# The first modulation of a two-block DiT on one core: whole row blocks of the weights, plain fp32 products on four column tiles

## The chip, the cores and the metric

The kernel runs on one core of a Trainium2 chip. Its engines are TensorE (PE in the profile; PEld are its weight loads), VectorE (DVE), ScalarE (ACT), GpSimd (POOL) and SyncE (SP), which here only issues DMAs. The metric is the device time of one execution in microseconds (us).

## The reference

Two transformer blocks over 256 tokens x and 256 context tokens, width 1024. Each block begins with a modulation: six vectors for x and six for the context, products of silu(c) and silu(c_ctx) with w_mod. The first two of the six (shift and scale) modulate the norms that go into the token mixer:

```
silu_c  = silu(c);  silu_cc = silu(c_ctx)                       # 1024 each
mod_x = silu_c  @ w_mod[l] + b_mod[l]                           # w_mod[l]: 1024 x 6144, fp32
mod_c = silu_cc @ w_mod[l] + b_mod[l]
sh1x, sc1x, g1x, sh2x, sc2x, g2x = split(mod_x, 6)
hx = rmsnorm(x, norm_mix_w[l])   * (1 + sc1x) + sh1x
hc = rmsnorm(ctx, norm_mix_w[l]) * (1 + sc1c) + sh1c
mx, mc = token_mixer(hx, hc, ...)                               # starts with hx @ w_in, hc @ w_in
x = x + g1x * mx;  ...                                          # then a dense channel mixer,
                                                                # and in block 1 eight experts, top 2
```

The change is about the first 2048 columns of mod_x and mod_c of block 0: a product of a 2 x 1024 matrix with 1024 x 2048 weights (8.4 MB), without which no token of block 0 can be modulated.

## The kernel before

Products that need the precision of fp32 are made of rounded parts. A load brings a unit of weights of 128 x 1024 numbers (0.5 MB) into one of four places `raw` (`load_unit`, line 128). `split_unit` then makes `hi` on ScalarE (a rounded copy, L145) and `lo` = raw - hi on VectorE (L149), in rings of three places each. The rounded type (fp32r) lets TensorE take a product in one pass; three such products (`mm3`, L156 to L158) stand for one exact one.

The first modulation (L309 to L345) goes by columns: four chunks of 512 columns, and in each four units of 256 rows. The two vectors are kept in `cst` as four columns per block of 128 rows, rounded part and rest of each, so that one product of `hi` and one of `lo` with them (L337) give four rows of 512 sums. ScalarE copies those four rows out (L338) into `rows`, whose fifth row is the bias. Four small products with a matrix of ones and zeros, `sel` (L341), add rows 0, 1, 4 and rows 2, 3, 4 and turn the result into columns, `colps`; VectorE copies these to `modc` (L344). From `modc` come the factors `ac` (L351), and then the norms of the tokens are transposed (L290) and modulated, block by block of 128 columns, on ScalarE (L300, L303, L304) and VectorE (L301, L305). The context's two tiles of tokens come first (`h_first[0]`), those of x (`xs`, scaled by L280) later, between the first products of the mixer. These blocks (`hb`, in the ring `rb`) are what the mixer multiplies with the weights w_in, starting with the gate inputs and keys (`gates_keys`, PE mm L156 to L158).

The order of instructions on each engine is set by a scheduler from the program's order, priorities and the waits that it expects; `split_unit` has high priority. `behind(a, b)` keeps a load behind another one in SyncE's queue: in this part all loads are a chain, w_mod first, then w_in, x and constants. The loads of SyncE and ScalarE share eight completion semaphores (the order's rows call them DMAHW0 to DMAHW7); a load waits for the one before it on the same semaphore. The later modulations (`mod_chunk`, from L399) work in another way, on VectorE (L417), with a sum over partitions by one fp32 product (L423, L427).

Other places in memory that matter here: the rings `rr` and `rb`, of four places of 128 x 2048 fp32 numbers each. In the first 40 us `rr` holds little (gate parameters, the start of the later modulations), and `rb` is unused until the modulated blocks go there.

Of the kernel before, what the change touches and what calls it, by code (L numbers as in the profile page):

```python
# [16 lines left out]
OP = mybir.AluOpType  # L17
# [21 lines left out]
def host_consts():  # L39
# [15 lines left out]
    sel = np.zeros((5, 2))  # L55
    sel[[0, 1, 4], 0] = 1
    sel[[2, 3, 4], 1] = 1
# [14 lines left out]
def hybrid_kernel(ctx: ExitStack, tc: tile.TileContext, a: dict, out: bass.AP, dbg=None, upto="end"):  # L72
# [10 lines left out]
    # before the experts' weights: raw units of w_mod, gates, sums; blocks of transposed tokens  # L83
    turn = {"mraw": 0, "blk": 0}

    def ring(kind, i, dt):
        """one of the rings' places of 8 KB"""
        return ringp.tile([128, 4, 512], dt, name=f"{kind}{i}", tag=f"{kind}{i}")
# [6 lines left out]
    def blk(dt=F32R):  # L95
        """half of a place; two in a row share one"""
        k = turn["blk"]
        turn["blk"] += 1
        if k % 2 == 0:
            turn["pair"] = ring("rb", k // 2 % 4, dt)  # L100
        assert turn["pair"].dtype == dt
        return turn["pair"][:, k % 2 * 2:k % 2 * 2 + 2]
# [5 lines left out]
    # ------------------------------------------------------------------ weights  # L108
# [3 lines left out]
    def place_of(x, n, keep=False):  # L112
        """the next place of a kind; the experts' units have rings of their own, with some places for once"""
# [23 lines left out]
    def chained():  # L137
        """the first loads and the last ones keep the order of the trace"""
        return W["chain"] or places
# [20 lines left out]
    # ------------------------------------------------------------------ constants  # L160
    # the scalar engine's function tables change in the order of the trace
# [7 lines left out]
    class InOrder:  # L169
        """the engine's instructions keep the order of the trace among themselves"""  # L170
# [50 lines left out]
    sel = consts.tile([5, 2], F32, name="sel")  # L221
# [9 lines left out]
    cst = consts.tile([128, KB, 4], F32R, name="cst")  # L231
# [6 lines left out]
    rows = mx0.tile([5, 2048], F32, name="rows", tag="uh")  # L238
    nc.scalar.dma_start(rows[4:5, :], a["b_mod"][0:1, 0:2048])
# [6 lines left out]
    def rstd_of(ss, pool, first=None):  # L246
        """(sum of ss / D + EPS) ** -0.5 for [128, 1], with a Newton step; first: the first half's EPS + ss / D"""
# [11 lines left out]
    def rstd_newton(ss, first, pool, i):  # L259
        """(ss / D + first) ** -0.5 for [128, 1]: Newton steps from an integer guess"""  # L260
# [13 lines left out]
    def norm_tile(xt, pool, bufs=2, junk=None):  # L274
        """rmsnorm without its weight; in place where the squares have a place of their own"""
# [7 lines left out]
    def h_steps(xns, blks, acol, bcol, pool, tr, h32tag, off=0, mix=(0, 1)):  # L283
        """Two token tiles -> modulated, transposed, split into blks[kb][:, :, seq half]."""
# [23 lines left out]
    # ------------------------------------------------------------------ first modulation  # L308
    with tc.high_priority():  # L309
# [3 lines left out]
        nc.vector.tensor_copy(cst[:, :, 0], cs[:, 0:8])  # L313
        nc.vector.tensor_tensor(cst[:, :, 1], cs[:, 0:8], cst[:, :, 0].bitcast(F32), op=OP.subtract)
        nc.vector.tensor_copy(cst[:, :, 2], cs[:, 8:16])
        nc.vector.tensor_tensor(cst[:, :, 3], cs[:, 8:16], cst[:, :, 2].bitcast(F32), op=OP.subtract)
# [3 lines left out]
    colps = ps0.tile([128, 512], F32, name="colps", tag="sc", bufs=4)[:, :32].rearrange("p (a b) -> p a b", b=2)  # L320
    modc = {}
    modc[0] = modp.tile([128, 2, 16], F32, name="modc0")
    for ch in range(4):
        if ch == 1:
            for t in range(2):
                ins = nc.sync.dma_start(xin[t], a["ctx"][0, t * 128:(t + 1) * 128, :]).ins
                behind(ins, W["load"])
                W["load"] = ins
            junk = mx0.tile([128, D], F32, name="junk", tag="v0")
            xns = [norm_tile(xin[t], mx0, junk=junk) for t in range(2)]  # L330
        mps = ps0.tile([128, 512], F32, name="mps", tag="mm", bufs=4)[:4]
        for q in range(4):
            hl = split_unit(load_unit(wsrc(a["w_mod"][0], q * 256, 2, ch * 512, 512), (2, 512)))
            for k in range(2):
                kb = 2 * q + k
                for i, m in enumerate(hl):
                    nc.tensor.matmul(mps, cst[:, kb, :], m[:, k, :], start=(kb == 0 and i == 0), stop=(kb == 7 and i == 1))  # L337
        nc.scalar.activation(rows[0:4, ch * 512:(ch + 1) * 512], mps, AF.Copy)  # L338
        for j in range(4):
            b = ch * 4 + j  # L340
            nc.tensor.matmul(colps[:, b, :], rows[:, b * 128:(b + 1) * 128], sel, start=True, stop=True)  # L341
        if ch % 2:
            s = ch // 2
            nc.vector.tensor_copy(modc[0][:, :, s * 8:(s + 1) * 8],  # L344
                                  colps[:, s * 8:(s + 1) * 8, :].rearrange("p b x -> p x b"))  # L345

    def acols(l, which, mc, x):
        """columns (a, b) of the modulated norm; mc [128, 2, 16]: shift | scale"""
# [37 lines left out]
    # ------------------------------------------------------------------ later modulations  # L386
    gp = {}

    class later:
        """instructions that give way to the next ones traced"""  # L390
# [10 lines left out]
    def mod_chunk(l, col, n_src, rows_out=None, cols_out=None):  # L401
        """512 columns of w_mod[l] from col, for x (and ctx): on the vector engine, with the
        sum over partitions left to the tensor engine."""
# [29 lines left out]
    def g_mod(l, which, n_src):  # L433
        col = (2 if which == 1 else 5) * D
        if (l, which) == (1, 2):
            # as columns; rows are made of them when they are needed
# [22 lines left out]
    # ------------------------------------------------------------------ token mixer  # L459
# [1176 lines left out]
```

## Time and profile before

| | before |
|---|---|
| time, median of 3 runs | 1826.84 us (1826.77 to 1829.52) |
| the profiled execution | span of 1826.0 us from first to last instruction; the page gives no other time of its own, so what lies around the span is taken as 0.84 us from the median |
| TensorE busy | 1782.2 us (98%) |
| VectorE busy | 1470.1 us (81%) |
| ScalarE busy | 1084.2 us (59%) |
| DMA | 479 MB, mean 262 GB/s |

Busy time is an average over stages with different limits; the start of the program, about 42 us until the first modulated block, is a stage of its own. A matmul's record is longer than its share of the engine, since matmuls are pipelined: the distance from one start to the next counts. An fp32 product is two records, a rounded one is one.

### The profile page before, as it was taken

To read this page: it belongs to the slowest core of one execution; us is meant where nothing else is said; L and a number is where in the kernel's file an instruction comes from. 1 tells how busy PE (TensorE), PEld (TensorE's weight loads), DVE (VectorE), ACT (ScalarE), POOL (GpSimd) and SP (SyncE) were. 2 spreads that over 40 slices of the span, in tenths; PEclk is the share of its full clock that TensorE was granted. 3 is DMA by queue.
4 is the path that set the end of the run, shared out by engine and by line. 5 is a ranking of instruction groups with operands and counts; after the bars stand their busy time and mean duration, and the time that the engine had idled before them with its cause. 6 is when DMAs were issued, how large, how long until landed. Compare 5 with 4: busy or idle time off the path is not lost.

```text
span 1826.0 us, 22994 instructions
## 1 busy us (share of the span) xinstructions
PE 1782.2 (98%) x8724; PEld 1450.5 (79%) x8724; DVE 1470.1 (81%) x1537; ACT 1084.2 (59%) x1120; POOL 26.8 (1%) x51
## 2 busy tenths in 40 slices
PE   6999999999999999999999999999999999999997
PEld 2777888888888887877888888888888888888875
DVE  6788896786565577668889888898898898988997
ACT  6733454222212366547777777777777777777774
POOL 1000000000000000000000000000000000000000
PEclk9999999999999999999999999999999999999999
DMA  8534374556555345469999999999999999999972
GB/s 289 188 94 133 106 247 137 183 174 184 185 187 183 116 130 185 150 249 359 334 352 338 349 363 354 344 369 342 366 362 338 366 359 339 364 348 360 335 236 97
DMA packets 253159, 478.99 MB, mean 262 GB/s; under 512 B 11773, under 2 KB 65279, under 8 KB 253039
## 3 DMA queue, kind: packets, MB, share of 16 engines
q1 hardware_dynamic: 251440, 473.80, 75.1%
q10 hardware_dynamic: 1040, 2.72, 0.4%
q8 instruction: 70, 1.15, 0.3%
q0 software_dynamic: 560, 0.92, 0.2%
q14 instruction: 49, 0.40, 0.1%
HBM read 476.35 MB, written 1.05 MB: 261 GB/s over the span
## 4 chain that ended last, share of the span: by engine, by line
PE 92%; DVE 3%; ACT 2%; DMA 1%; issue 1%; ACTq 0%; DVEq 0%; POOLq 0%
PE h L1479 11%; PE h L1482 11%; PE h L1478 11%; PE mm L156 8%; PE mm L157 8%; PE mm L158 8%; PE y L156 8%; PE y L157 8%; PE y L158 8%; PE sc L1340 1%; PE sc L1460 1%; PE sc L584 1%; ACT hi L145 1%; PE mm L427 1%; DMA raw<-w_mod 1%
## 5 line engine op out<-in xcount | busy, mean ns | idle before, releaser
L177 DVE TENSOR_TENSOR rb<-raw,rb 128x2048 fp32r<-128x2048 f32 (+1 forms) x159 | 355.3, 2246 | 16.6 <-PE h L1479 11.0
L177 ACT ACTIVATE rb<-raw 128x2048 fp32r<-128x2048 f32 (+1 forms) x159 | 300.1, 1887 | 100.2 <-PE h L1482 65.6
L1479 PE MATMUL h<-rb,hg 128*128 128x512 f32 x896 | 351.4, 392 | 1.2 <-DVE rb L177 1.2
L145 ACT ACTIVATE hi<-raw 128x1024 fp32r<-128x1024 f32 x143 | 151.2, 1059 | 331.9 <-PE mm L157 100.7
L1478 PE MATMUL h<-rb,hg 128*128 128x512 f32 x670 | 262.9, 392 | 0.0
L149 DVE TENSOR_TENSOR lo<-raw,hi 128x1024 fp32r<-128x1024 f32 x143 | 174.7, 1223 | 103.8 <-ACT hi L145 102.4
L177 DVE TENSOR_TENSOR rb<-raw,part 128x2048 fp32r<-128x2048 f32 (+1 forms) x80 | 177.7, 2221 | 34.5 <-ACT part L177 21.4
L1479 PEld LDWEIGHTS h<-rb,hg 128*128 128x128 f32 x896 | 168.4, 188 | 38.8 <-DVE rb L177 3.8
L417 DVE SCALAR_TENSOR_TENSOR rr<-rr,cs,rr 128x512 f32<-128x512 f32 x256 | 181.8, 747 | 10.5 <-DMA rr<-b_mod 6.6
L1482 PE MATMUL h<-rb,hg 128*128 128x512 f32 x670 | 179.8, 390 | 1.6 <-DVE hg L177 1.6
L157 PE MATMUL y<-rb,ht 128*128 128x512 f32 x448 | 177.4, 396 | 0.0
L177 ACT ACTIVATE part<-raw 128x2048 fp32r<-128x2048 f32 (+1 forms) x80 | 148.9, 1861 | 34.3 <-PE y L158 33.3
L156 PE MATMUL mm<-hbk,hi 128*128 128x512 f32 (+1 forms) x456 | 167.3, 368 | 0.1
L157 PE MATMUL mm<-hbk,hi 128*128 128x512 f32 (+1 forms) x456 | 164.9, 362 | 1.1 <-DVE hbk L305 1.1
L158 PE MATMUL mm<-hbk,lo 128*128 128x512 f32 (+1 forms) x456 | 165.0, 362 | 0.0
L177 DVE TENSOR_TENSOR rb<-rr,rb 128x2048 fp32r<-128x2048 f32 (+1 forms) x68 | 150.0, 2208 | 11.9 <-ACT h L177 7.9
L177 ACT ACTIVATE rb<-rr 128x2048 fp32r<-128x2048 f32 (+1 forms) x68 | 126.3, 1857 | 38.9 <-PE h L1482 22.7
L1482 PEld LDWEIGHTS h<-rb,hg 128*128 128x128 f32 x670 | 125.7, 188 | 28.3 <-DVE hg L177 2.1
L1478 PEld LDWEIGHTS h<-rb,hg 128*128 128x128 f32 x670 | 125.9, 188 | 26.2 <-issue 0.2
L157 PEld LDWEIGHTS y<-rb,ht 128*128 128x128 f32 x448 | 84.3, 188 | 19.5 <-DVE rb L177 0.3
L156 PEld LDWEIGHTS mm<-hbk,hi 128*128 128x128 f32 x456 | 85.7, 188 | 16.5 <-issue 1.2
L157 PEld LDWEIGHTS mm<-hbk,hi 128*128 128x128 f32 x456 | 85.9, 189 | 16.0 <-DVE hbk L305 1.3
(355 smaller groups left out, 3143.8 us busy)
## 6 DMA issues: line engine op xcount, KB each, us to landing
raw<-moe_w SPq DMA_DIRECT2D x228, 1024.0 KB
rr<-moe_w SPq DMA_DIRECT2D x96, 1024.0 KB
rr<-w_mod SPq DMA_DIRECT2D x80, 512.0 KB
raw<-ffn_w SPq DMA_DIRECT2D x72, 512.0 KB
raw<-w_in SPq DMA_DIRECT2D x32, 512.0 KB
raw<-w_out SPq DMA_DIRECT2D x23, 512.0 KB
raw<-w_mod SPq DMA_DIRECT2D x16, 512.0 KB
raw<-moe_w SPq DMA_DIRECT2D x11, 512.0 KB
```

The costliest lines, as they stand in the source:

```text
L145: ins = nc.scalar.activation(hi, raw, AF.Copy).ins
L149: nc.vector.tensor_tensor(lo, raw, hi.bitcast(F32), op=OP.subtract)
L156: nc.tensor.matmul(ps, lh, rh, start=start, stop=False)
L157: nc.tensor.matmul(ps, lh, rl, start=False, stop=False)
L158: nc.tensor.matmul(ps, ll, rh, start=False, stop=stop)
L177: r = getattr(self.engine, name)(*args, **kw)
L417: nc.vector.scalar_tensor_tensor(accs[x], rv[:, k, :], cs[:, x * 8 + kb:x * 8 + kb + 1], accs[x], op0=OP.mult, op1=OP.add)
L427: nc.tensor.matmul(ps[:, j:j + 1], accs[x][:, j * 128:(j + 1) * 128], ones[:, 0:1], start=True, stop=True)
L584: nc.tensor.matmul(P[r][:, t, c, :], kf(r * 64, c, t), qf(r * 64, c, t), start=True, stop=True)
L1478: nc.tensor.matmul(H[i], hgh[:, kb, :], hi[:, j, :], start=(kb == 0), stop=False)
L1479: nc.tensor.matmul(H[i], hgh[:, kb, :], lo[:, j, :], start=False, stop=False)
L1482: nc.tensor.matmul(H[i], hgl[:, kb, :], hi[:, j, :], start=False, stop=(kb == 7))
```

## The change

The weights of the first modulation are loaded by rows: eight blocks of 128 rows and 2048 columns, 1 MB each, into places of the rings `rr` (0 to 2) and `rb` (3, 0, 1, 2 and 3 again). They are not rounded. TensorE multiplies them as they are, in fp32, with the two vectors (`cst` has two fp32 columns per block instead of four rounded ones). Per block there are four products of 512 columns each, one per group of columns; each writes two rows of its own 32 partitions of one bank, so each uses another tile of 32 columns of the array. After the eighth block ScalarE and VectorE copy two of the four groups each into `rows`, which has 128 partitions now: three rows in use per group (x, context, bias, the bias by four small loads) and zeros elsewhere, set by GpSimd. Four products with the larger `sel` turn all into columns, and one copy makes `modc`. Everything is in the diff below, from which only removed comments and the like are left out.

```diff
@@ -52,9 +52,11 @@
-    sel = np.zeros((5, 2))
-    sel[[0, 1, 4], 0] = 1
-    sel[[2, 3, 4], 1] = 1
+    sel = np.zeros((128, 4, 2))
+    for c in range(4):
+        sel[[32 * c, 32 * c + 2], c, 0] = 1
+        sel[[32 * c + 1, 32 * c + 2], c, 1] = 1
...
-    sel = consts.tile([5, 2], F32, name="sel")
+    sel = mx0.tile([128, 4, 2], F32, name="sel", tag="A", bufs=6)
...
-    cst = consts.tile([128, KB, 4], F32R, name="cst")
+    cst = consts.tile([128, KB, 2], F32, name="cst")
...
-    rows = mx0.tile([5, 2048], F32, name="rows", tag="uh")
-    nc.scalar.dma_start(rows[4:5, :], a["b_mod"][0:1, 0:2048])
+    rows = mx0.tile([128, 512], F32, name="rows", tag="uh")
+    nc.gpsimd.memset(rows, 0.0)
+    for c in range(4):
+        nc.scalar.dma_start(rows[32 * c + 2:32 * c + 3, :], a["b_mod"][0:1, c * 512:(c + 1) * 512])
...
-        nc.vector.tensor_copy(cst[:, :, 0], cs[:, 0:8])
-        nc.vector.tensor_tensor(cst[:, :, 1], cs[:, 0:8], cst[:, :, 0].bitcast(F32), op=OP.subtract)
-        nc.vector.tensor_copy(cst[:, :, 2], cs[:, 8:16])
-        nc.vector.tensor_tensor(cst[:, :, 3], cs[:, 8:16], cst[:, :, 2].bitcast(F32), op=OP.subtract)
+        nc.vector.tensor_copy(cst, cs.rearrange("p (x k) -> p k x", x=2))
...
-    for ch in range(4):
-        if ch == 1:
+
+    mps = ps0.tile([128, 512], F32, name="mps", tag="mm", bufs=4)
+
+    def load_next(dst, src):
+        ins = nc.sync.dma_start(dst, src).ins
+        behind(ins, W.get("load"))
+        W["load"] = ins
+
+    for kb in range(KB):
+        if kb == 2:
             for t in range(2):
-                ins = nc.sync.dma_start(xin[t], a["ctx"][0, t * 128:(t + 1) * 128, :]).ins
-                behind(ins, W["load"])
-                W["load"] = ins
+                load_next(xin[t], a["ctx"][0, t * 128:(t + 1) * 128, :])
             junk = mx0.tile([128, D], F32, name="junk", tag="v0")
             xns = [norm_tile(xin[t], mx0, junk=junk) for t in range(2)]
-        mps = ps0.tile([128, 512], F32, name="mps", tag="mm", bufs=4)[:4]
-        for q in range(4):
-            hl = split_unit(load_unit(wsrc(a["w_mod"][0], q * 256, 2, ch * 512, 512), (2, 512)))
-            for k in range(2):
-                kb = 2 * q + k
-                for i, m in enumerate(hl):
-                    nc.tensor.matmul(mps, cst[:, kb, :], m[:, k, :], start=(kb == 0 and i == 0), stop=(kb == 7 and i == 1))
-        nc.scalar.activation(rows[0:4, ch * 512:(ch + 1) * 512], mps, AF.Copy)
-        for j in range(4):
-            b = ch * 4 + j
-            nc.tensor.matmul(colps[:, b, :], rows[:, b * 128:(b + 1) * 128], sel, start=True, stop=True)
-        if ch % 2:
-            s = ch // 2
-            nc.vector.tensor_copy(modc[0][:, :, s * 8:(s + 1) * 8],
-                                  colps[:, s * 8:(s + 1) * 8, :].rearrange("p b x -> p x b"))
+        place = spots[kb % 4] if kb < 3 else ring("rb", kb % 4, F32)
+        raw = place.rearrange("p a b -> p (a b)")
+        load_next(raw, a["w_mod"][0, kb * 128:(kb + 1) * 128, 0:2048])
+        for c in range(4):
+            nc.tensor.matmul(mps[32 * c:32 * c + 2], cst[:, kb, :], raw[:, c * 512:(c + 1) * 512],
+                             start=(kb == 0), stop=(kb == 7))
+    for c in range(4):
+        rc = slice(32 * c, 32 * c + 2)
+        if c % 2:
+            nc.vector.tensor_copy(rows[rc], mps[rc])
+        else:
+            nc.scalar.activation(rows[rc], mps[rc], AF.Copy)
+    colps = small(None)[:, :32]
+    for j in range(4):
+        nc.tensor.matmul(colps[:, j * 8:(j + 1) * 8], rows[:, j * 128:(j + 1) * 128],
+                         sel.rearrange("p c x -> p (c x)"), start=True, stop=True)
+    nc.vector.tensor_copy(modc[0].rearrange("p x (c j) -> p x c j", j=4),
+                          colps.rearrange("p (j c x) -> p x c j", j=4, c=4))
```

The scheduler orders the start of the program anew; behind the first products of the mixer the order on VectorE, ScalarE and TensorE is as before. Two places matter. The first is ScalarE ahead of the first modulated block (`h`); `hi<-raw` are roundings, `rows<-mps` the copies of the modulation, `wl` the gate weights of w_in. Before, from the rounding of the last unit but two on:

```order
L145 ACTIVATE hi<-raw 128x1024 [waits DMAHW2_49,DVE_49,PE_49]
L145 ACTIVATE wl<-rr_65 128x256 [waits DMAHW3_49]
L145 ACTIVATE hi<-raw 128x1024 [waits DMAHW4_49,DVE_49,PE_49]
L338 ACTIVATE rows<-mps 4x512 [waits PE_49]
L145 ACTIVATE hi<-raw 128x1024 [waits DMAHW5_49,DVE_49]
L303 ACTIVATE h_344<-sc,modc_118,ac_333 128x256 [waits DVE_49]
```

And now (line numbers are those of the changed kernel, where L147 is the rounding, L348 the copy, L282 the squares of a tile of x and L307 the first modulated block):

```order
L147 ACTIVATE wl<-rr_65 128x256 [waits DMAHW6_49]
L348 ACTIVATE rows<-mps 2x512 [waits PE_49]
L147 ACTIVATE hi<-raw 128x1024 [waits DMAHW7_49]
L348 ACTIVATE rows<-mps 2x512 [waits DVE_49]
L147 ACTIVATE hi<-raw 128x1024 [waits DMAHW0_49]
L282 ACTIVATE junk,ss<-xs 128x1024 [waits DMAHW1_49]
L197 ACTIVATE rsy<-ss,epsc 128x1 [waits Activation_49]
L307 ACTIVATE h_214<-sc,modc_118,ac_203 128x256 [waits DVE_49,PE_49]
```

The two copies stand behind the gate weights and one unit of w_in, and the first block also behind a second unit and the squares of x. The second place is SyncE's queue. Before, its first loads were (a `raw` place is free when VectorE has subtracted):

```order
L128 DMA raw<-w_mod 128x2x512 x3
L128 DMA raw<-w_mod 128x2x512 [waits DMAHW0_49]
L326 DMA xs<-ctx 128x1024 [waits DMAHW3_49]
L326 DMA xs<-ctx 128x1024 [waits DMAHW4_49]
L128 DMA raw<-w_mod 128x2x512 [waits DMAHW5_49,DVE_49]
L128 DMA raw<-w_mod 128x2x512 [waits DMAHW6_49,DMAHW2_49,DVE_49]
```

And now:

```order
L327 DMA rr_64<-w_mod 128x2048
L327 DMA rr_65<-w_mod 128x2048
L327 DMA xs<-ctx 128x1024 [waits DMAHW3_49]
L327 DMA xs<-ctx 128x1024 [waits DMAHW5_49]
L327 DMA rr_66<-w_mod 128x2048 [waits DMAHW6_49]
L327 DMA rb_161<-w_mod 128x2048 [waits DMAHW7_49]
L327 DMA rb_167<-w_mod 128x2048 [waits DMAHW0_49]
L327 DMA rb_173<-w_mod 128x2048 [waits DMAHW3_49]
L327 DMA rb_179<-w_mod 128x2048 [waits DMAHW4_49]
L327 DMA rb_185<-w_mod 128x2048 [waits DMAHW7_49,DMAHW5_49,PE_49]
L130 DMA rr_65<-w_in 128x8x32 [waits DMAHW6_49]
L130 DMA raw<-w_in 128x4x256
```

The waits for VectorE (DVE) are gone from these loads; the eighth block alone waits for an engine, TensorE, and the first load of w_in for `raw` waits for nothing but its turn.

## Rows read from the trace of the kernel before

**Rows 1.** The page: span, engines' busy time, and the chain's shares by engine.

```profile
span 1826.0 us, 22994 instructions
...
PE 1782.2 (98%) x8724; PEld 1450.5 (79%) x8724; DVE 1470.1 (81%) x1537; ACT 1084.2 (59%) x1120; POOL 26.8 (1%) x51
...
PE 92%; DVE 3%; ACT 2%; DMA 1%; issue 1%; ACTq 0%; DVEq 0%; POOLq 0%
```

**Rows 2.** Chain of waits, first 60 us: start us, us, what.

```profile
6.70 5.18 DMA prow<-gla_norm_w
...
36.54 1.71 PE mps L337 x4
...
38.67 1.76 PE mps L337 x7
40.46 0.59 ACT rows L338
41.09 1.06 PE colps L341 x8
42.18 0.18 DVE modc L344
...
42.67 0.56 ACT h L303
...
46.48 6.91 DMA rr<-w_mod
...
56.88 0.78 PE mm L156 x4
```

**Rows 3.** Stretches: us, busy of each engine, TensorE's clock, DMA share, GB/s.

```profile
0.00:13.50 13.50, 2.87 (x8) 0.90 (x9) 5.56 (x12) 5.34 (x6) 6.33 (x16) 1.00 0.87 306
3.00:6.00 3.00, 0.00 (x0) 0.00 (x0) 0.15 (x1) 1.06 (x1) 2.42 (x6) 1.00 1.02 390
13.50:30.00 16.50, 13.43 (x60) 5.23 (x58) 12.50 (x20) 13.50 (x21) 0.00 (x0) 1.00 0.81 260
30.00:34.00 4.00, 2.23 (x9) 0.60 (x9) 2.39 (x4) 2.31 (x3) 0.00 (x0) 1.00 1.01 330
34.00:40.00 6.00, 6.00 (x28) 3.54 (x27) 4.74 (x5) 3.50 (x5) 0.00 (x0) 0.72 0.94 305
44.00:57.00 13.00, 11.15 (x89) 10.09 (x90) 11.76 (x30) 10.91 (x28) 0.00 (x0) 1.00 0.90 316
57.00:98.00 41.00, 41.00 (x243) 31.98 (x242) 26.99 (x42) 27.14 (x52) 0.00 (x0) 1.00 0.42 129
98.00:131.00 33.00, 31.94 (x208) 24.89 (x209) 32.63 (x53) 11.56 (x18) 1.05 (x2) 1.00 0.33 96
131.00:800.00 669.00, 661.35 (x3424) 542.73 (x3421) 482.45 (x748) 263.36 (x420) 16.94 (x31) 1.00 0.52 164
```

**Rows 4.** ScalarE and VectorE by line, first 45 us; the last rounding in time order.

```profile
L149 DVE TENSOR_TENSOR lo<-raw,hi 128x1024 fp32r<-128x1024 f32 x18 | 21.9, 1224 | 10.7 <-ACT hi L145 10.7
L145 ACT ACTIVATE hi<-raw 128x1024 fp32r<-128x1024 f32 x18 | 18.9, 1053 | 12.7 <-DMA raw<-w_mod 8.6 <-PE mps L337 3.8
L278 ACT ACTIVATE junk<-xs 128x1024 f32<-128x1024 f32 x2 | 2.1, 1042 | 0.0
...
37.88 1.06 ACT L145 ACTIVATE hi<-raw 128x1024 fp32r<-128x1024 f32 x1 [0.78 <-PE mps L337]
```

**Rows 5.** Plain fp32 products: by line (mean ns), and pieces of the chain.

```profile
L423 PE MATMUL mm<-rr,sqc 128*128 128x512 f32 x12 | 5.8, 592 | 0.0
...
86.65 1.99 PE sc L584 x32
94.41 2.85 PE sc L584 x32
100.27 0.86 PE sc L423 x2
...
879.36 1.78 PE sc L1340 x16
```

More of the change, by code (lines that the diff above doesn't have):

```diff
@@ L319, in hybrid_kernel @@
     nc.vector.tensor_copy(pcol, pps)
-    colps = ps0.tile([128, 512], F32, name="colps", tag="sc", bufs=4)[:, :32].rearrange("p (a b) -> p a b", b=2)
     modc = {}
     modc[0] = modp.tile([128, 2, 16], F32, name="modc0")
-    for ch in range(4):
-        if ch == 1:
+    mps = ps0.tile([128, 512], F32, name="mps", tag="mm", bufs=4)
[5 more added lines that the diff above has]
+        if kb == 2:
```

## The prediction

> **What bounds the kernel now.** I read the page first: TensorE is busy 98% of the span and the chain that ends last is 92% TensorE [rows 1], so time is won only where TensorE waits or does less. The change touches the first modulation, so next came the chain of waits of the first 60 us [rows 2]. There the reader sees a start that TensorE doesn't set: a small load until 11.9 (6.70 + 5.18), then loads, roundings and subtractions in turn, until the modulation's columns are copied at 42.18 and the first modulated block begins at 42.67 (h L303). The stretches [rows 3] say why it takes so long: the DMA moves 390 GB/s while its queue is full (3 to 6), but 260 from 13.5 to 30, because a load waits for one of four places and a place is free only after its rounding (1,053 ns) and its subtraction (1,224 ns) [rows 4]. Behind the start TensorE is busy 41.00 of 41 us from 57 to 98, VectorE 32.63 of 33 from 98 to 131, and then TensorE 661 of 669 up to 800: each waits for work, not for a clock time, so a start that comes earlier by some us should move everything behind it by nearly as much.
>
> The sum is made against the profiled span, 1826.0 [rows 1]. The median of the runs is 1826.84, so 0.84 lies around the span and I carry it along unchanged. A measurement of this kernel tells about 0.2%, 3.65 us, from no change.
>
> **Part 1, the loads.** Before, 16 units of 0.52 MB wait for places; now 8 blocks of 1.05 MB go to eight uses of seven other places. Only the last block waits for a product (the fourth block's, same place). The bytes ahead of the end of block 8 are 8 x 1.049 + 1.049 (two context tiles) + 0.20 (identity, ones) = 9.64 MB. The first 13.5 us of before move 306 GB/s x 13.5 = 4.13 MB [rows 3]; there the queue was full, so I keep that start. The other 5.51 MB take 14.1 us at 390 GB/s, or 16.7 at the 330 of 30 to 34. The ends are 27.6 and 30.2; I take 28.5, near the full queue's row, since nothing but lanes of earlier small loads holds these issues back. Before, the last unit's rounding starts at 37.88 [rows 4].
>
> The Trainium skill (DMA: Bandwidth & Descriptors, Bandwidth) puts about 358 GB/s as the limit of memory for one core; the trace is above that with 390. By the page the blocks would end at 13.5 + 5.51 / 0.358 = 28.9, by the row at 27.6.
>
> **Part 2, what goes.** 16 roundings (16 x 1.05 = 16.8 us of ScalarE) and 16 subtractions (16 x 1.22 = 19.6 us of VectorE) [rows 4]. Both lie in a stretch where these engines only serve the modulation, so they are worth the delay they put into the loads and no more. ScalarE no longer holds the gla_norm_w load behind the silu: before, TensorE stood for it until 11.9 (6.70 + 5.18 us to land) [rows 2]; now it is issued in the first microseconds with the loads ahead of it, and with the same 5.18 to land products begin at about 8.
>
> **Part 3, the products.** 64 rounded products of 512 columns go, at 0.25 us apart when the clock is full (1.76 for 7) and 0.43 when it is half (1.71 for 4) [rows 2]. In their place stand 32 plain fp32 products. One such product with 512 columns takes 0.86 us on the full array (two records) [rows 5], so 4 x 0.86 = 3.42 a block and 27.4 for all if the column tiles don't overlap. No product of before uses column tiles. Nearest are the scores, whose two row tiles alternate in the same way: 16 products of 128 columns take 1.99 us in one place and 2.85 in another, where 8 products of that size on the full array take 1.78, 16 thus 3.56 [rows 5]. Overlap is therefore worth 3.56 / 1.99 = 1.8 or 3.56 / 2.85 = 1.25. The block then costs 1.9 or 2.7 us; with all four tiles at once it would be 0.86. A block arrives every 1.049 / 0.39 = 2.7 us, so between 0.86 and 2.7 the loads stay the bound, and at 3.42 the products become it. I take 1.9, the row with plain operands: the last product ends at 28.5 + 1.9 = 30.4.
>
> The Trainium skill (TensorE: Matmul & The Clock Gate, Measured speedup vs the span model) gives 2.38 times for three column tiles of 512 columns. By that a block would cost about 3.42 / 2.38 = 1.4 us, an estimate from the page, and the last product would end 0.5 us sooner; no run here shows column tiles.
>
> **Part 4, from the products to the columns.** This part takes some of it back. ScalarE now has the rounding of the gate weights and of the first two units of w_in in front of and between its two copies, and VectorE the two subtractions before the columns; all of these were issued behind the copies or beside the products before. Their data follow block 8 in the same queue: 0.13 + 0.52 MB make unit 1 land at about 30.3, unit 2 at 31.8 (0.36 MB/us). Step by step: copy 0, 30.4 to 31.0 (0.59, the row copy of before [rows 2]); rounding of unit 1 to 32.1; copy 2 to 32.7; VectorE subtracts unit 1 to 33.3 and copies the last rows to 33.9 (I take 0.6 again); the four selecting products 1.06 [rows 2] to 35.0; the columns 0.18, but behind the subtraction of unit 2 (rounded by 33.8, subtracted by 35.1) to 35.3; the factors 0.3 (42.67 - 42.18 - 0.18) to 35.6. ScalarE meanwhile squares the first tile of x (1.04 [rows 4], landed by 33.5) and takes its logarithm, to 35.2. So the first modulated block begins at about 35.8 against 42.67: 6.9 us. With the loads at 30.2 and 2.7 a block it would be 38.3 (4.4 us); with 27.6 and 0.86 a block the roundings still stand there, and it would be about 34.5 (8.2 us).
>
> **Part 5, behind it.** Two things differ. The clock: TensorE now stands from 30.4 to 34, and a granted 0.72 (34 to 40 [rows 3]) came in before after a stretch with 2.23 of 4 us busy. The 16 transposes and the first products of the mixer could run at 1.2 GHz for a while; a stretch like that one costs 6 x 0.28 = 1.7 us of work at the full 2.4 GHz. I charge 1.0 (ends 0 and 1.7). The norm of x: its first tile is now squared ahead of the blocks, which takes 1.04 us [rows 4] and two short instructions off ScalarE between the context's blocks and those of x. Before, TensorE starts on x at 56.88 after VectorE's scaled tile [rows 2]; VectorE is nearly full there, 11.76 of 13 [rows 3], with four sums of the next modulation between, so only about half of that comes through: 0.4 to 0.7 us gained, as 0.4. The two roundings of w_in in Part 4 were due before the mixer anyhow and aren't counted again. From 57 on the engines' order is the same as before, and nothing in it depends on the clock time.
>
> The sum: 6.9 - 1.0 + 0.4 = 6.3 us. 1826.84 - 6.3 = **1820.5 us**. Own range of this case: 1818 to 1823.5, from 8.2 + 0.4 and 4.4 - 1.0.
>
> **Rivals.** (1) *The column tiles don't overlap.* For it: every fp32 product on the full array shows 0.86, and no row shows column tiles. Against it: the row tiles' 1.8. Products then run from 8 to about 8 + 27.4 + 1.7 (such a stretch of half clock at first) = 37.1, the copies and the rest of Part 4 end at about 42.4, and the gain is 0.3 + 0.4 to 1: 1826.0, no change.
> (2) *The start comes earlier but half is lost.* For it: the chain has 6.91 us on the load of the next modulation's weights, landing at 53.39, ahead of the scaled x tile [rows 2]; this load now stands behind the masks, whose place is freed by the selecting products. Against it: those end at 35.0 and the queue is full until about 36.5, so the load lands at about 40, before VectorE asks for it. Gain 3: 1823.9.
> (3) *Slower: the tiles neither overlap nor pipeline*, because each of a product's two records must be through before the next tile's starts. A record of 512 columns alone takes 592 ns [rows 5]; 64 x 0.59 = 37.9 us, from 8 to 46, at half clock towards 76. The blocks begin at 51, 8.6 later than now: 1835 (to 1860). It decides from about 4 us a block on. Against it: all rows of fp32 products, in line or on row tiles, are pipelined.
> (4) *It doesn't do what it says*, the scheduler having put other work into the cleared stretch: the orders of ScalarE and VectorE show this for the two units of w_in, which is in Part 4 already.
>
> **Chances.** Forecast 0.65, tiles with weak overlap (the 4.4 end, 1823.5) 0.10, (1) 0.10, (2) 0.07, (3) 0.08. Faster by over 0.2%, which is below 1823.2: nearly all of the forecast, half of the weak overlap, a little of (2), 0.70. Within 0.2%: the rest of these and most of (1), 0.20. Slower: (3) and a tail of (1), 0.10. The range of 8 in 10 is 1817 to 1827: it takes in the best end with a little room, the weak overlap, (2) and (1), and leaves (3) out.
>
> **What would show it.** Right: in the changed profile the DMA stays near 380 GB/s from 3 to 35 us; the last block lands at 28 to 30; the four products of a block take about 1.9 us; the blocks begin at 35 to 38; from 60 us on every stretch looks as before, 6 us earlier. Wrong: TensorE busy without a gap from 8 to 37 (rival 1); ScalarE waiting for a load of w_in between two copies by more than 1 us; a half clock in the mixer's first 8 us; the x blocks not earlier than 52 (rival 2).

## The result and the profile after

The changed kernel takes 1841.92 us (median; 1840.54 to 1844.32) against 1827.16 for the kernel before on the same chip: a ratio of 1.0080, 95% interval 1.0066 to 1.0094. It is 14.8 us slower; the prediction was 1820.5, with 1827 as the end of its range. The profiled execution is at the upper end of these runs: span 1842.3, against 1826.0.

The page of the changed kernel, in the lines of [rows 1]: TensorE is busy 14.8 us more, the other large engines less.

```profile
span 1842.3 us, 22881 instructions
...
PE 1797.0 (98%) x8700; PEld 1449.4 (79%) x8700; DVE 1452.3 (79%) x1519; ACT 1067.4 (58%) x1102; POOL 27.3 (1%) x52
```

**The start did come earlier.** The chain of its first 60 us (start us, us, what), which answers [rows 2]:

```profile
1.71 7.94 DMA sel<-k_sel
9.66 0.33 SPq L327
...
19.64 1.93 PE mps L341 x8
21.58 8.18 DMA rb<-w_mod
29.80 1.04 PE mps L341 x8
30.84 4.34 issue
35.18 1.85 PE sc L351 x8
37.03 3.51 PE sc L294 x16
...
52.17 0.77 PE mm L158 x4
```

The last block is there at 29.80, its four products (eight records) take 1.04 us, the selecting products begin at 35.18, and TensorE is on x at 52.17 instead of 56.88: 4.7 us earlier. The first modulated block begins at 38.01 instead of 42.67, also 4.7. One execution tells such a lead to about 2 us only: the same start gives 40.81 for the kernel before in experiment 5, and 38.55 for the changed kernel in experiment 4. The stretches that answer [rows 3] (us, busy time of each engine, TensorE's granted clock, DMA share, GB/s) show a hole in the loads from 8 to 10 us, a fuller queue behind it, and half clock from 34 to 40:

```profile
0.00:13.50 13.50, 5.12 (x18) 0.84 (x18) 1.88 (x6) 2.83 (x4) 5.81 (x15) 1.00 0.69 243
8.00:10.00 2.00, 1.86 (x2) 0.09 (x2) 0.01 (x1) 0.00 (x0) 0.50 (x2) 1.00 0.23 55
13.50:30.00 16.50, 9.43 (x47) 0.64 (x48) 2.80 (x10) 3.10 (x8) 0.98 (x2) 0.69 1.03 409
34.00:40.00 6.00, 4.82 (x23) 4.85 (x24) 3.71 (x10) 4.22 (x9) 0.00 (x0) 0.50 0.79 261
```

**The loss is in the experts, 800 us behind the change.** The products that make h, one row for each kernel (count; shortest/median/longest record in ns; first and last start in us), before and after:

```profile
L1479 PE MATMUL h<-rb,hg x896: 387/389/793, 813.6 to 1797.1; 128*128 128x512 f32 x180
```

```profile
L1488 PE MATMUL h<-rb,hg x896: 390/397/798, 812.7 to 1813.3; 128*128 128x512 f32 x180
```

From the first to the last are 983.5 us before and 1000.6 after. So 17.1 us are lost there, and only 0.9 us of the early start is left at the first of them; 17.1 - 0.9 = 16.2 is nearly all of the 16.3 between the two spans. The instructions of this stretch and their order are the same, TensorE is busy all the time (996.52 us of 1000 from 800 to 1800 before, 996.64 after) at a granted clock of 1.00 in both, and the DMA moves 343 and 341 GB/s. What differs is the pace of the products. Four of them in a row as one piece of the chain, before and after:

```profile
1201.55 0.91 PE h L1482 x4
```

```profile
1207.54 0.94 PE h L1491 x4
```

That is not one slow place: of the pieces of four between 900 and 1700 us, 176 of 181 take 0.91 before and all take 0.93 or 0.94 after. From start to start the records give a mean of 227 ns before and 234 after. There are 2688 h products: 896 + 670 + 670 on the rows that show rb as the weights, 226 + 226 on those that show part. 2688 x 7 ns = 18.8 us, about the size of the loss.

**What had moved.** The pools are filled from the left side upwards, in the order of the code, and from the right side downwards. cst lost 64 bytes per partition (8 x 4 x 4 before, 8 x 2 x 4 now), and sel, in a place of 32 bytes, went to another pool. Every tile behind them on the left stands 96 bytes lower: the rings rr and rb and the experts' weights. The tokens hg, on the right, stay. Modulo 256, weights and hg were both at 32; now the weights are at 192. The experiments ask whether this is what the products feel.

### The profile page after: what moved, and what is told of

The parts are those of the page before. It is cut to its first block, busy times and chain, and to the rows that moved or that the text cites. A ratio compares the mean times of both kernels' runs of the same rounds, so it can differ in the third digit from the quotient of the medians.

```text
span 1842.3 us, 22881 instructions
## 1 busy us (share of the span) xinstructions
PE 1797.0 (98%) x8700; PEld 1449.4 (79%) x8700; DVE 1452.3 (79%) x1519; ACT 1067.4 (58%) x1102; POOL 27.3 (1%) x52
## 4 chain that ended last, share of the span: by engine, by line
PE 92%; DVE 3%; ACT 2%; DMA 2%; issue 1%; SPq 0%; ACTq 0%; DVEq 0%
PE h L1488 11%; PE h L1491 11%; PE h L1487 11%; PE mm L158 8%; PE mm L159 8%; PE mm L160 8%; PE y L158 8%; PE y L160 8%; PE y L159 8%; PE sc L1349 1%; PE sc L1469 1%; PE sc L593 1%; DMA rb<-w_mod 1%; PE mm L436 1%; PE sc L698 1%
## 5 line engine op out<-in xcount | busy, mean ns | idle before, releaser
L1488 PE MATMUL h<-rb,hg 128*128 128x512 f32 x896 | 357.2, 399 | 1.1 <-DVE rb L179 1.0
L147 ACT ACTIVATE hi<-raw 128x1024 fp32r<-128x1024 f32 x127 | 134.4, 1059 | 321.7 <-PE mm L159 100.5
L1487 PE MATMUL h<-rb,hg 128*128 128x512 f32 x670 | 266.8, 398 | 0.0
L151 DVE TENSOR_TENSOR lo<-raw,hi 128x1024 fp32r<-128x1024 f32 x127 | 155.3, 1224 | 96.6 <-ACT hi L147 94.7
L1491 PE MATMUL h<-rb,hg 128*128 128x512 f32 x670 | 184.5, 396 | 1.6 <-DVE hg L179 1.6
L158 PE MATMUL mm<-hbk,hi 128*128 128x512 f32 (+1 forms) x456 | 167.7, 369 | 0.1
L158 PEld LDWEIGHTS mm<-hbk,hi 128*128 128x128 f32 x456 | 85.8, 189 | 17.0 <-issue 1.2
```

What stands on the lines that cost most here:

```text
L147: ins = nc.scalar.activation(hi, raw, AF.Copy).ins
L151: nc.vector.tensor_tensor(lo, raw, hi.bitcast(F32), op=OP.subtract)
L158: nc.tensor.matmul(ps, lh, rh, start=start, stop=False)
L1487: nc.tensor.matmul(H[i], hgh[:, kb, :], hi[:, j, :], start=(kb == 0), stop=False)
L1488: nc.tensor.matmul(H[i], hgh[:, kb, :], lo[:, j, :], start=False, stop=False)
L1491: nc.tensor.matmul(H[i], hgl[:, kb, :], hi[:, j, :], start=False, stop=(kb == 7))
```

## The experiments

Each pad below is a tile of that many bytes behind epsc in the constants, with a VectorE memset of its first column; the instructions and their order are otherwise those of the kernel it is added to. With ratios stands the 95% interval. "Distance" is the address of the moving operand (weights) less that of the stationary one, modulo 256, from the places that the compiler gave the tiles.

**1. The 96 bytes put back into the changed kernel.**

```diff
     epsc = consts.tile([128, 1], F32, name="epsc")
+    pad = consts.tile([128, 24], F32, name="pad")
+    nc.vector.memset(pad[:, 0:1], 0.0)
```

> The changed kernel with 96 unused bytes per partition added to the constants, so that the rings and all weight places lie at the byte addresses they had before (they lie 96 bytes lower in the changed kernel, because cst and sel shrank); nothing else moves. Theory (addresses): the products of the experts' first layer (h) start every 234 ns in the changed kernel and every 227 before, 2688 records x 7 ns = 19 us, because of where weights and tokens lie to each other; with the pad they go back to 227, and the time is 1842 - 19 = 1823, 4 us faster than before, since the first block begins 4.7 us earlier. Rival (order of the rb ring, whose place 3 now lies lowest, or anything else of the changed start that lasts, as its clock): the pad changes nothing, 1842, h at 234.

Measured: 1823.27 us, ratio 0.9982 (0.9972 to 0.9991). The experts take what they took before, 983.4 us from first to last, and the lead of the start, 3.6 us at the blocks (39.11) and at x (53.32 against 56.88), is there at the first h product (813.6 to 810.0) and at the end (span 1822.4).

```profile
L1490 PE MATMUL h<-rb,hg x896: 387/389/793, 810.0 to 1793.4; 128*128 128x512 f32 x180
...
1200.85 0.91 PE h L1493 x4
```

So the change itself gains 0.2%, and 18.7 us between the two medians hang on 96 unused bytes.

**2. The kernel before with 416 bytes more** (416 = 256 + 160, the distance of the changed kernel), **512 and 256 more.** The edit is the same, with 104, 128 and 64 columns.

> The kernel before with 416 unused bytes added to the constants: rings and weight places move up by 416 = 512 - 96 bytes, the tokens (hg) of the experts stay. Theory (addresses, by their distance modulo 512): the same distance as in the changed kernel, h at 234 ns, 1827 + 19 = 1846. Rival (the changed start is the cause): 1827, h at 227.

> The kernel before with 512 unused bytes: every address of the weights moves, but not modulo 512. Theory: no change, 1827, h at 227. Rival (any move from the old addresses costs, or a larger period such as 1024 or 2048 counts): slower, up to 1846.

> The kernel before with 256 unused bytes: weights and tokens then lie at distance 256 modulo 512 and 0 modulo 256. If the period is 256 or less: 1827, h at 227. If it is 512: slower, h at about 234, 1846. I lean to 512 with 0.5: products of two tiles at equal addresses modulo 128 (hi and rb in block 0) are slow before, which rules out 128.

Measured: 1844.08 (ratio 1.0098, 1.0081 to 1.0114), 1826.87 (1.0002, 0.9993 to 1.0012) and 1825.94 (0.9996, 0.9986 to 1.0006). The loss comes without any part of the change, and a shift by 256 or 512 has none. The h products with 416 bytes more take what they take in the changed kernel:

```profile
L1481 PE MATMUL h<-rb,hg x896: 390/397/798, 812.7 to 1813.3; 128*128 128x512 f32 x180
```

**3. 128 bytes more**, 32 columns.

> The kernel before with 128 unused bytes per partition among its constants, so that every tile on the left side, the experts' weights among them, stands 128 bytes higher, and the stationary tokens (hg) stay where they were. Theory (a product runs at 227 ns only where its moving and stationary operand have the same address modulo 256): modulo 256 the two are 128 bytes apart, the h products of the experts come every 231 to 234 ns instead of 227, 2688 of them, so 11 to 19 us longer: 1838 to 1846 us. Rival (the period is 128 bytes or less): the two are still in step, the products stay at 227 ns and the time at 1826 to 1828 us.

Measured: 1837.26 us, ratio 1.0069 (1.0054 to 1.0085). If the pace goes by the addresses with a period, 128 is not one and 256 is. The h products come every 232 ns, so a little less is lost than at a distance of 160:

```profile
1206.62 0.92 PE h L1484 x4
...
L157 PE MATMUL y<-rb,ht 128*128 128x512 f32 x448 | 175.6, 392 | 0.0
```

The second line is from the y products, the experts' second layer, which have ht as the stationary operand. This pad brings them from a distance of 192 to one of 64, and from start to start they take 229.5 ns on average here instead of 233.4. On average that is nearly as quick as in step (228.9, experiment 5), so pace is not a matter of in step or not alone. It also settles the sum: 2688 h products lose 14.0 us, 1344 y products win back about 5, and from the first to the last h product the kernel takes 8.3 us more. Another 2.1 us are lost before the experts (see Part 5 below).

**4. The changed kernel as it is, with hg moved after the weights.**

```diff
             HT[e, c] = sil = mo.tile([128, 512], F32, name="sil", tag="sil", bufs=2)
+            if not padded:
+                padded.append(mo.tile([128, 24], F32, name="pada"))
+                nc.vector.memset(padded[0][:, 0:1], 0.0)
```

> The changed kernel as it is, with 96 unused bytes in front of the sil and ht tiles, in the pool that stands above hg: ht stays where it is and hg (the tokens, the stationary operand of the h products) moves 96 bytes down, as the change had moved the weights. The left side, the weights among it, stands where the changed kernel has it. Theory (what counts is the distance of the two operands modulo 256): h products at 227 ns again, 18.8 us less than the changed kernel: 1823. Rival (the weights' own address is what makes the products slow, for its writers or for the transfers): h stays at 234 ns and the time at 1842.

Measured: 1825.07 us, ratio 0.9987 (0.9978 to 0.9996). The weights stand where the changed kernel has them, and the products are fast again (sil moves along with hg, but no h product reads it):

```profile
L1492 PE MATMUL h<-rb,hg x896: 387/389/791, 811.3 to 1795.5; 128*128 128x512 f32 x180
...
1202.36 0.91 PE h L1495 x4
```

For the h products it is the distance of the two operands that counts, not the weights' own address, and not who writes or loads them.

**5. The kernel before with ht moved into step.** The stationary operand ht stands at 96 modulo 256 in all kernels so far; the weights stand at 32 in the kernel before, so the distance is 192.

```diff
             HT[e, c] = sil = mo.tile([128, 512], F32, name="sil", tag="sil", bufs=2)
+            if not padded:
+                padded.append(mo.tile([128, 48], F32, name="pada"))
+                nc.vector.memset(padded[0][:, 0:1], 0.0)
...
             HT[e, c] = ht
+            if len(padded) == 1:
+                padded.append(mo.tile([128, 16], F32, name="padb"))
+                nc.vector.memset(padded[1][:, 0:1], 0.0)
```

> The kernel before with 192 unused bytes in front of the two ht tiles and 64 behind them, in the pool of the experts: ht (the stationary operand of the y products) moves from 96 to 32 modulo 256, where the weights stand too, and hg moves by a whole 256 bytes. Nothing else is changed but two VectorE memsets of one column. Theory (the address rule): the y products, which take 233 ns from start to start in every kernel so far, fall to 227; 1344 of them by 6.4 ns are 8.6 us, so about 1818 us, with the h products still at 227. Rival (the y products are slow for a reason of their own, such as their accumulation or their outputs): they stay at 233 and the time at 1827 us.

Measured: 1820.59 us, ratio 0.9977 (0.9967 to 0.9988): faster than both kernels, by 5.6 us instead of 8.6. The y products by line (busy us, mean ns of a record), before and with ht moved:

```profile
L157 PE MATMUL y<-rb,ht 128*128 128x512 f32 x448 | 177.4, 396 | 0.0
L156 PE MATMUL y<-rb,ht 128*128 128x512 f32 x228 | 90.5, 418 | 0.0
...
L158 PE MATMUL y<-part,ht 128*128 128x512 f32 x220 | 87.0, 396 | 0.0
L156 PE MATMUL y<-part,ht 128*128 128x512 f32 x220 | 82.4, 396 | 0.0
```

```profile
L157 PE MATMUL y<-rb,ht 128*128 128x512 f32 x448 | 175.0, 391 | 0.0
L156 PE MATMUL y<-rb,ht 128*128 128x512 f32 x228 | 90.3, 417 | 0.0
...
L158 PE MATMUL y<-part,ht 128*128 128x512 f32 x220 | 85.7, 390 | 0.0
L156 PE MATMUL y<-part,ht 128*128 128x512 f32 x220 | 80.9, 389 | 0.0
```

Three of these four groups follow the rule (5 to 7 ns a record); the 228 of L156 on rb do not (418 to 417), nor do the 228 of L158 on rb (395 to 394, not shown). Together 888 of the 1344 y products become faster, and 888 x 6.4 ns = 5.7 us is the gain measured. Why the others don't is open: their operands stand in step too, so the distance is not all there is.

**6. The hole in the loads.** In the chain above SyncE's third load stands for sel until 9.66 (in experiment 1 its fifth stands for a load of prow until 10.69). Here, with the 96 bytes put back, sel, prow and rows are loaded on GpSimd's queue.

```diff
-    nc.scalar.dma_start(sel, a["k_sel"])
+    nc.gpsimd.dma_start(sel, a["k_sel"])
...
-        nc.scalar.dma_start(rows[32 * c + 2:32 * c + 3, :], a["b_mod"][0:1, c * 512:(c + 1) * 512])
+        nc.gpsimd.dma_start(rows[32 * c + 2:32 * c + 3, :], a["b_mod"][0:1, c * 512:(c + 1) * 512])
```

> The changed kernel with the 96 bytes put back (measured at 1823.3 us), and the eight small loads of the start (sel, the three of prow, the four of rows) issued by GpSimd's queue instead of ScalarE's; only the two loads of crow stay. Theory (SyncE's third load waits in the changed kernel for a semaphore that a small load holds, and the loads stand still from about 8 to 10 us): the hole goes, the first 13.5 us move about 300 GB/s instead of 249, 0.7 MB more, which at 400 GB/s is 1.7 us; the last block of w_mod lands about 1.7 us earlier (30.9 to 29.2), and the end comes up to 1.7 us earlier: about 1821.5. Rival 1: the hole goes and the last block lands earlier, but the gain is given back before the mixer's end, 1823.3. Rival 2: the small loads through the other queue are late themselves (rows or prow after 29 us) and hold the selecting products: 1824 or more.

Measured: 1821.77 us, ratio 0.9976 (0.9966 to 0.9986). SyncE issues without a stop, 8 to 10 us move 376 GB/s where the kernel of experiment 1 moves 42, the last block is there at 27.80 (30.91 in experiment 1), and the first modulated block begins at 36.01 instead of 39.11. Of these 3.1 us, 1.1 reach the end by the ratios (0.9982 there, 0.9976 here) and 1.8 by the spans (1822.4 and 1820.6).

```profile
8.00:10.00 2.00, 1.86 (x2) 0.09 (x2) 0.00 (x0) 1.05 (x1) 1.14 (x3) 1.00 1.05 376
...
3.47 13.90 DMA rb<-w_mod
...
27.80 1.04 PE mps L343 x8
28.84 4.34 issue
```

**7. One addition in place of the four copies**, again with the 96 bytes put back.

```diff
-    for c in range(4):
-        rc = slice(32 * c, 32 * c + 2)
-        if c % 2:
-            nc.vector.tensor_copy(rows[rc], mps[rc])
-        else:
-            nc.scalar.activation(rows[rc], mps[rc], AF.Copy)
+    nc.vector.tensor_tensor(rows, mps, brow, op=OP.add)
```

> The changed kernel with the 96 bytes put back (measured at 1823.3 us), and one VectorE addition over 128 partitions (PSUM, cleared early, plus the bias rows) in place of the four copies of two rows that alternate between ScalarE and VectorE with roundings between them; sel has the bias row no more, and the bias is loaded twice (eight loads of 2 KB instead of four). Theory (the 4.3 us between the last product and the selecting products are those copies and the roundings that the engines do between them): the addition takes about 0.7 us and the gap falls to about 1 us; the first modulated block comes 3 us earlier, and if all of it reaches the end, 1820.2 us. Rival: the gap falls as said, but the roundings of w_in that the copies stood among, and the clock at half until about 42 us, then set the mixer's pace, and less than 1 us of it reaches the end: 1822.3 to 1823.3.

Measured: 1822.81 us, ratio 0.9982 (0.9973 to 0.9991), no more than experiment 1 within the interval. The 4.3 us fall to 0.8 as expected, but the last products come 1.3 us later (32.17; whether the four loads more are the reason was not tested), and x begins only 1.4 us earlier (51.95). By the spans 2.1 us reach the end (1822.4 and 1820.3), by the ratios nothing. The chain now runs over a load of the masks, which the selecting products let go, and the rounded blocks.

```profile
32.17 1.08 PE mps L346 x8
33.33 0.70 DVE rows L348
34.08 1.89 PE sc L351 x8
35.98 4.03 DMA mkr<-k_masks
...
51.95 0.77 PE mm L158 x4
```

**8. All of it together**: experiments 1, 5, 6 and 7 on the changed kernel, the bias's eight loads on GpSimd's queue.

> All edits together on the changed kernel: the 96 bytes among the constants, ht moved into step with the weights, the small loads of the start on GpSimd's queue (the bias as eight), and the one addition in place of the four copies. By the single runs against 1826.9 to 1826.2 of before: 96 bytes -3.3 us, ht -5.6, small loads -1.5, one addition -0.5 to -2: 1814 to 1816 us if they add up. Rival (the two edits of the start give back what they gain, since the clock or the loads of w_in then set the mixer's pace): 1817 to 1818.

Measured: 1813.99 us (1811.09 to 1816.26), ratio 0.9927 (0.9913 to 0.9941): faster than both kernels. By the ratios the edits alone give 3.3 us (experiment 1), 4.2 (5), and 1.1 and 0 on top of experiment 1 (6 and 7), 8.6 in all, each with an interval of about 2 us either way; together they give 13.3. By the spans the single edits give 3.6, 7.2, 1.8 and 2.1, 14.7 in all, and together 15.4, so that the edits help each other is not shown at the end. At the start they may: edits 6 and 7 alone bring x 3.0 and 1.4 us earlier than experiment 1 has it, together 5.9, with the first modulated block at 32.39 and x at 47.39. That is 1.5 us more, no more than starts of one kernel differ by:

```profile
27.87 1.08 PE mps L346 x8
29.03 0.70 DVE rows L348
...
32.39 0.56 ACT h L311
...
47.39 0.78 PE mm L158 x4
```

## Why the prediction was wrong

**The step that failed is Part 5's last sentence, "From 57 on the engines' order is the same as before, and nothing in it depends on the clock time".** The order is the same, and a shift in time is harmless: in experiment 1 the start's 3.6 us reach the end whole, as the sentence at the head of the prediction has it (a start that comes earlier "should move everything behind it by nearly as much"). But the same instructions in the same order are not the same work when their tiles have moved. The change to cst and sel was read as a change of the first modulation; its 96 bytes moved all tiles behind them, and with them every product of the experts. No rival said so either: rival 3, the slower one, placed its loss in the first 50 us. Experiments 1, 2 and 4 show the cause from three sides: bytes put back, bytes added without the change, the other operand moved.

**Part 1, the loads: 29.80, within 27.6 to 30.2, but not by its reason.** "There the queue was full, so I keep that start" failed: 243 GB/s against 306 in [rows 3], for the hole from 8 to 10 us. What it named and cost at nothing, the "lanes of earlier small loads", was that hole; experiment 6 prices it at 3.1 us of the start and 1 to 2 of the end. The rest went faster than reckoned, 409 GB/s from 13.5 to 30 against 390. The Trainium skill (DMA: Bandwidth & Descriptors, Bandwidth) has about 358 GB/s as one core's limit; this row is above it, as that of before was.

**Part 2** is as said for the loads, which no longer wait for roundings. That the products begin at 8.1 us (predicted: about 8) is luck: one product, which needs nothing of prow, goes ahead of the transposition of prow. That one, for which the 8 was reckoned, comes at 10.53, 7.0 us after the issue of gla_norm_w at 3.5 and not 5.18, and the other products follow it at 10.74.

**Part 3, the products: cheaper than said.** A block takes 1.04 us at full clock and 1.93 in the half-clock stretch at 19.64, not 1.9 at full clock: the four column tiles run beside each other nearly as if they were one product (0.86 in [rows 5]; 4 x 0.86 / 1.04 = 3.3 times). Row tiles were the wrong neighbour. By the Trainium skill (TensorE: Matmul & The Clock Gate, Measured speedup vs the span model), with 2.38 times for three tiles, a block would take about 1.4 us, an estimate; the trace has less. Rivals 1 and 3 are out with this row.

**Part 4, from products to columns: mis-sized by 1.8 us.** The block was to begin at 35.8 and begins at 38.01, 2.2 later; 0.4 of it comes from the products ahead. The copies and roundings came in the order described. In order of time (start us, us; the last bracket is the wait ahead), ScalarE and VectorE of the changed kernel:

```profile
30.91 0.59 ACT L348 ACTIVATE rows<-mps 2x512 f32<-2x512 f32 x1
...
31.59 0.69 DVE L346 COPY rows<-mps 2x512 f32<-2x512 f32 x1 [0.19 <-ACT rows L348]
32.04 1.06 ACT L147 ACTIVATE hi<-raw 128x1024 fp32r<-128x1024 f32 x1 [0.54 <-DMA raw<-w_in]
33.12 0.59 ACT L348 ACTIVATE rows<-mps 2x512 f32<-2x512 f32 x1
...
34.38 0.70 DVE L346 COPY rows<-mps 2x512 f32<-2x512 f32 x1
```

The last copy ends at 35.08, 1.2 later than the predicted 33.9: besides the 0.4, the rounding waits 0.5 for its load. The other 1.0 us is the clock: the selecting products take 1.85 instead of 1.06 us, and the transposes of the context run at the same half clock ahead of the first block.

**Part 5, the clock and x.** The half clock was charged with 1.0 us behind the blocks; it stood already ahead of them, from 34 to 40 in the stretch above. x gained 4.7 us, as much as the blocks, not 0.4 more. It begins at 52.17, which the forecast had named as the sign of rival 2 ("not earlier than 52"), but no load stands in the chain ahead of it: rival 2's mechanism did not come. Of these 4.7 us the changed kernel keeps 0.9 at 813 us. Two rows before and after, and one of the kernel with 416 bytes more, show where it is lost (first and last start in us):

```profile
L689 PE MATMUL sc<-ch,S x64: 271/272/374, 200.1 to 766.5; 64*128 64x128 f32 x64
...
L156 PE MATMUL mm<-hbk,hi x456: 277/389/799, 272.9 to 737.1; 128*128 128x512 f32 x110, 128*128 128x256 f32 x42
```

```profile
L698 PE MATMUL sc<-ch,S x64: 272/272/374, 196.2 to 765.8; 64*128 64x128 f32 x64
...
L158 PE MATMUL mm<-hbk,hi x456: 277/392/793, 271.1 to 736.4; 128*128 128x512 f32 x110, 128*128 128x256 f32 x42
```

```profile
L156 PE MATMUL mm<-hbk,hi x456: 274/392/793, 271.0 to 736.4; 128*128 128x512 f32 x110, 128*128 128x256 f32 x42
```

3.9 us of lead at 196, 1.8 at 271, 0.7 at 736. Two things are in this. Between 196 and 271 TensorE of the changed kernel waits 1.04 us at 242, and its clock then falls to half for a while. That is not the work of the addresses: experiment 4, with the same order and the same places up to the experts, waits 0.17 us there and takes 72.5 us between these two rows instead of 74.9; the kernel before with 512 bytes more, at the old addresses modulo 256, waits 0.92, falls to half as well and takes 74.7 (72.8 before). What brings the wait in one execution and not in another is open. The products behind it, in the changed kernel and with 512 bytes more (the last bracket is the wait):

```profile
242.40 1.02 PE L436 MATMUL sc<-sqc,rr 128*128 128x1 f32 x8 [1.04 <-issue]
```

```profile
245.97 1.02 PE L429 MATMUL sc<-sqc,rr 128*128 128x1 f32 x8 [0.92 <-issue]
```

The 1.1 us between 271 and 736 do go with the addresses. From first to last this row takes 464.2 us at the old addresses modulo 256 (before, 512 bytes more, experiment 1), 465.3 or 465.4 with the left side 96 bytes lower modulo 256 (the changed kernel, experiment 4, 416 bytes more), and 466.3 with 128 bytes more.

**The sum.** Predicted were -6.3. By the profiled executions: -4.7 at the start, +3.8 on the way to the experts, +17.1 in them, +0.1 behind them, +16.3 in all (+14.8 by the medians). With the 96 bytes put back it is -3.6 by the spans, 1823.3 by the median: the own range of the forecast, 1818 to 1823.5, holds that number at its upper end. Of the 6.3 forecast about 3 are not there even without the moved tiles: in that kernel's execution the products end at 31.95 instead of 30.4, and the block begins 3.3 later than reckoned, 1.8 of it in Part 4.

## What to carry to other kernels

Before a change to a small tile is counted as local, look at what stands behind it in its pool: if the large operands of a later, TensorE-bound stage move, its products can change their pace with every instruction in its place. A loss that is spread evenly over products that the change doesn't touch is best tested by putting the bytes back, before any theory of the edit itself. And where products bound a kernel, try to bring each pair of operands into step (here: same address modulo 256) with a few unused bytes; in this kernel that was worth 5.6 us for ht and 18.7 us for hg. Measure it: of the y products with ht a third did not follow.

## What the runs showed of the hardware that was not expected

- The experts' products of 128x512 on the full array start every 227 ns where the two operands are at the same address modulo 256, every 229.5 ns on average at a distance of 64 (ht), and every 232 to 234 ns at the other distances tried, 128 and 160 for hg, 96 and 192 for ht; all at a granted clock of 1.00. The exception is two groups of 228 y products (experiment 5), which stay slow in step. What in the chip has this period no run here tells.
- Four column tiles of fp32 products, two rows and 512 columns each, take 1.04 us together; one product on the full array takes 0.86 [rows 5].
- A load of 4 KB in 128 pieces, issued at 1.71 us beside loads of 1 MB, held SyncE's next load until 9.66 by the chain; with eight small loads, this one among them, on another queue the same stretch moves 376 GB/s instead of 42 (55 in the changed kernel).
